# Spare weight tiles opened first, sixteen wide units inside a two-bank first part, fewer gathers in the projection, and a cheaper one-hot and id step in a decoder layer

## The chip, the cores and the metric

One core of one Trainium2 chip runs the kernel. The metric is device microseconds of an execution, the median of several runs. An execution of the program before takes 4138.65 us.

## What is computed

One decoder layer on 512 tokens of width 2048, all in float32: an RMS norm, two kinds of attention (16 heads each) with gates, a projection back to the residual, and a product-key expert layer. The parts that the change is about:

```
merged = concat(y_a, y_b) * sigmoid(gates)                  # 512 x 4096, 32 heads of 128
x  = x + merged @ w_out                                     # w_out 4096 x 2048
h  = rms_norm(x, ffn_norm_g)
q  = h @ w_peer_q                                           # 8 expert heads, two halves of 128 each
s1, i1 = top_k(q[first half]  @ sub_keys, 16)               # over 128 keys
s2, i2 = top_k(q[second half] @ sub_keys, 16)
cand = s1[:, None] + s2[None, :]                            # 16 x 16 candidates
top, pos = top_k(cand, 16);  expert = 128 * i1[..] + i2[..] # one of 16384 experts
g  = softmax(top);  a = u[expert] . h                       # u, v: 16384 x 2048
x  = x + sum over the 8 * 16 experts of (g * gelu(a)) * v[expert]
```

## The kernel before, in words

A float32 product runs as three matmuls of a rounded high part and a rest (`mm3`, lines L137 to L139). Each weight is loaded by SP in tiles of 512 KB (`load`, L101). A tile has two halves of 128x512. Of each half ACT writes the high part (`half_hi`, L108) and DVE the rest (`half_lo`, L113). Tiles live in a pool of three raw buffers, and `spare` opens two or more raw buffers beside them, with output tiles of their own. Pools are stacked in memory, so what a pool lies over depends on what was opened before it.

*Phase 1* norms the input, projects, and runs 32 attention heads. The last head's gate is stored to a scratch tensor in HBM by SP (`mrg`, L320).

*Phase 2* is the projection by w_out, in units of one half tile each. `out0_units` makes 128 narrow units for token block 0 (three matmuls of 512 columns each). `out_units` makes 128 wide units for blocks 1 to 3 (nine matmuls each), the list `main`. The list of units is run in order, the next half prepared while one is multiplied (`run`, with `LOOK`). The order is: the narrow units with `FEW` = 4 wide ones among the last of them; the norm of block 0 (L732 is its first DVE instruction), `WAIT` = 6 wide units, the query projection of block 0 with one wide unit after every 8 of its 64 units; then `select` for block 0, and the other wide units. From there on expert rows of block 0 are gathered. Each half adds `RATE` to a credit, and a full credit issues a gather: an indirect DMA of 128 rows of 8 KB by POOL (L952) into one of three buffers, and a product with a sum on DVE (L954). The last `REST` wide units come without gathers. After each issue a scheduler decides where an instruction goes in its engine's order.

*Phase 3* norms blocks 1 to 3 (hb, L872), transposes them (L878), splits them (L94, L95), projects the queries and selects the experts, four times (`select`). Within `select`, per half, an is_equal of 1536 elements (L839), a multiplication with the ids (L841) and a sum (L843) turn the chosen positions into ids. The last of the four is followed by nine transposes into `lists` (L1018). During the last part the first 32 units of the up projection run (`up_stream`, 12 matmuls of 336 columns each): 14 rows of 4 units are made ahead.

*Phase 4* treats 336 tokens of blocks 1 to 3 by dense products over all experts. `gate_matrix` builds the gate matrix in 84 groups of four tokens. Per group `pick` writes four one-hot rows for the first id (a three-row is_equal, L1029, and one tensor_scalar, L1031, that multiplies by the gate at once), four for the second id (L1033), and ACT scales three rows (L1035). PE multiplies (L1048), ACT copies (L1049), and every fourth group POOL copies (L1051). `LEFT` = 21 up units are spread over the groups, and 3 more follow. Its order on PE, DVE, ACT and POOL is written by hand. Then a stream of 948 weight halves carries the other up units, the down units and the gathers that are left: 352 in all.

Of the kernel before, what the change touches and what calls it, by code (L numbers as in the profile page):

```python
# [19 lines left out]
P = 128  # L20
SEQ = 512
# [45 lines left out]
RATE = 0.46  # L67
REST = 10
# [5 lines left out]
FEW = 4  # L74
# [3 lines left out]
LEFT = 4 * AHEAD - FIRST - 3  # L78
# [3 lines left out]
class Kern:  # L82
# [437 lines left out]
    def phase1(self):  # L520
        tc, nc, a = self.tc, self.nc, self.a
        with self.pool(name="hT", bufs=1, side="right") as hp, self.pool(name="keep", bufs=1) as keep, \
# [9 lines left out]
            with self.pool(name="xin", bufs=1) as xp:  # L532
# [8 lines left out]
                for k in range(KD):  # L541
# [3 lines left out]
                                                   op0=OP.mult, op1=OP.subtract)  # L545
                    a_, eng = (accp, nc.gpsimd) if k % 2 else (acc, nc.vector)
# [17 lines left out]
    def phase2(self, res, sm):  # L564
# [12 lines left out]
        with self.pool(name="mgr", bufs=1) as self.mgr, self.pool(name="msp", bufs=3) as self.msp, \  # L577
                self.pool(name="tka", bufs=1) as tk, self.spare(NRAW2, NSP2), \
# [109 lines left out]
    def out0_units(self, tk, main):  # L688
# [14 lines left out]
        def unit(w, c, q, u, k2):  # L703
            k = q * 8 + 2 * u + k2
            if k == 0:
                ps[c] = (self.pa if c < 2 else self.accp).tile([P, SEQ], F32, name="pa" if c < 2 else "acc")
# [4 lines left out]
        def some(qs):  # L711
            return [self.piece(a["w_out"][q, c, u], k2, st, lambda w, c=c, q=q, u=u, k2=k2: unit(w, c, q, u, k2))
                    for c in range(4) for q in qs for u in range(4) for k2 in range(2)]
# [5 lines left out]
        early, late = some(range(3)), some([3])  # L719
# [3 lines left out]
        out = early[:40] + [self.bare(own)] + early[40:64] + half(0) + early[64:] + [self.bare(bring, 3)]  # L723
        for i in range(0, len(late), 8):
            out += late[i:i + 8] + main[i // 8:i // 8 + 1] + (half(1) if i == 8 else [])
        return out
# [78 lines left out]
    def select(self, tk, vals, ids, n, gt, ie, eqs):  # L805
# [4 lines left out]
        nc.vector.tensor_copy(idf, ids)  # L810
        cand = tk.tile([P, n, NC // 8, 8], F32, name="cand")
# [25 lines left out]
        nc.vector.tensor_tensor(out=pf[:, 1], in0=slot, in1=w, op=OP.add)  # L837
        for c, eq in enumerate(eqs):
            nc.vector.tensor_tensor(out=eq, in0=pf[:, c, :, :, None].to_broadcast(bc),  # L839
                                    in1=iota[:, None, None, :].to_broadcast(bc), op=OP.is_equal)  # L840
            nc.vector.tensor_tensor(out=eq, in0=eq, in1=idf[:, c, :, None, :].to_broadcast(bc), op=OP.mult)  # L841
        for c, eq in enumerate(eqs):
            nc.vector.tensor_reduce(out=ie[:, c], in_=eq.rearrange("p (t h) a b -> p t h a b", t=nt), op=OP.add, axis=AX)  # L843
# [165 lines left out]
    def gate_matrix(self, pool, acc, ahead):  # L1009
        nc = self.nc  # L1010
        lists = pool.tile([P, 3, TD], F32, name="lists")
        for b in range(ND):
            for j in range(3):
# [4 lines left out]
                nc.scalar.copy(lists[:, j, b * P + o - NX:b * P + P - NX], tp[:, o:])  # L1018
# [270 lines left out]
```

## Time and profile before

| | |
|---|---|
| median of three runs | 4138.65 us (4133.84 to 4142.6) |
| the profiled execution | 4135.6 us, of which 4133.8 us is the span |
| PE busy | 4026.1 us (97%), 22575 matmuls |
| DVE busy | 3140.7 us (76%) |
| ACT busy | 1897.5 us (46%) |
| POOL busy | 644.4 us (16%) |
| DMA | 937.94 MB, mean 227 GB/s |

The span runs from the first to the last instruction of the trace. A stage of the program is found in it by the names of its instructions: the last head ends and the narrow units begin near 1454 us, block 0's norm is at 1587, the first hb at 1914, the end of the last `select` at 2151, the gate matrix from 2162 to 2287, and the stream of phase 4 after that. Busy shares are an average over stages with different limits, so the stages are read one by one. A window's row gives busy time of each engine, the granted TensorE clock as a share of 2.4 GHz, and what the DMA engines moved.

### The profile page before, as it was taken

What the parts mean: (1) busy time and instruction counts of PE and PEld (TensorE: products, weight loads), DVE (VectorE), ACT (ScalarE), POOL (GpSimd) and SP (SyncE); (2) the same over time, 40 slices, a digit from 0 to 9 for tenths busy, and PEclk for the clock granted to TensorE, in tenths of its full rate; (3) what the DMA queues carried; (4) which work ended last, traced back from release to release, by engine and by line L of the source; (5) the groups of instructions that cost most, each with busy time, mean ns of one, the idle gap of its engine ahead of it and who ended that gap; (6) DMA issues with size and microseconds to landing.
All of it is one profiled execution on the core that took longest, in us unless ns stands there. A gap on an engine that the chain in (4) does not pass through costs nothing. (4 is left out here: it accounts for less than half of the span.)

```text
span 4133.8 us, 61120 instructions
## 1 busy us (share of the span) xinstructions
PE 4026.1 (97%) x22575; PEld 3637.5 (88%) x22575; DVE 3140.7 (76%) x5379; ACT 1897.5 (46%) x3677; POOL 644.4 (16%) x531
## 2 busy tenths in 40 slices
PE   8999999999999989998999999999999999999999
PEld 6888888888888757787999999999999999999998
DVE  8555655655565567898999888888888888888886
ACT  4555555555555565433349433333333333333332
POOL 1111101111111100021001112112222222122220
PEclk9999999999999989998999999999999999999999
DMA  3222222222222377698337898989989989899896
GB/s 133 90 77 82 81 86 82 82 79 86 86 82 79 107 278 259 246 354 309 108 108 222 325 343 329 346 330 350 341 329 340 345 335 344 344 325 357 319 342 215
DMA packets 246925, 937.94 MB, mean 227 GB/s; under 512 B 23761, under 2 KB 70865, under 8 KB 197841
## 3 DMA queue, kind: packets, MB, share of 16 engines
q1 hardware_dynamic: 190944, 550.11, 38.3%
q0 software_dynamic: 52160, 375.94, 24.0%
q10 hardware_dynamic: 3520, 7.98, 0.6%
q8 instruction: 177, 2.90, 0.3%
q14 instruction: 124, 1.01, 0.1%
HBM read 895.75 MB, written 38.14 MB: 226 GB/s over the span
## 5 line engine op out<-in xcount | busy, mean ns | idle before, releaser
L108 ACT CAST whi<-raw 128x512 fp32r<-128x512 f32 x1820 | 1110.2, 621 | 1730.6 <-PE acc L138 604.2
L113 DVE TENSOR_TENSOR wlo<-raw,whi 128x512 fp32r<-128x512 f32 x1820 | 1219.6, 687 | 512.7 <-ACT whi L108 481.0
L137 PE MATMUL acc<-Wh,whi 128*128 128x336 f32 x2048 | 643.2, 318 | 5.7 <-DVE x L1124 3.0
L138 PE MATMUL acc<-Wl,whi 128*128 128x336 f32 x2048 | 645.1, 316 | 0.0
L137 PE MATMUL a<-dh,whi 128*128 128x336 f32 x1984 | 629.2, 317 | 0.8 <-issue 0.6
L138 PE MATMUL a<-dl,whi 128*128 128x336 f32 x1984 | 626.5, 316 | 0.0
L139 PE MATMUL a<-dh,wlo 128*128 128x336 f32 x1984 | 621.2, 316 | 0.6 <-DVE wlo L113 0.6
L139 PE MATMUL acc<-Wh,wlo 128*128 128x336 f32 x2048 | 608.5, 318 | 11.3 <-DVE wlo L113 10.8
L137 PE MATMUL mm<-hh,whi 128*128 128x512 f32 x1424 | 571.6, 402 | 8.6 <-ACT hh L543 8.6
L138 PE MATMUL mm<-hl,whi 128*128 128x512 f32 x1424 | 571.1, 401 | 4.3 <-DVE hl L544 4.0
L139 PE MATMUL mm<-hh,wlo 128*128 128x512 f32 x1424 | 569.9, 401 | 0.0
L137 PEld LDWEIGHTS acc<-Wh,whi 128*128 128x128 f32 x2048 | 385.4, 189 | 9.3 <-issue 5.7
L139 PEld LDWEIGHTS acc<-Wh,wlo 128*128 128x128 f32 x2048 | 376.1, 189 | 17.8 <-DVE wlo L113 17.5
L138 PEld LDWEIGHTS acc<-Wl,whi 128*128 128x128 f32 x2048 | 386.9, 189 | 0.0
L137 PEld LDWEIGHTS a<-dh,whi 128*128 128x128 f32 x1984 | 372.6, 188 | 2.2 <-issue 1.7
L138 PEld LDWEIGHTS a<-dl,whi 128*128 128x128 f32 x1984 | 372.8, 188 | 0.0
L139 PEld LDWEIGHTS a<-dh,wlo 128*128 128x128 f32 x1984 | 371.2, 188 | 1.1 <-DVE wlo L113 1.1
L138 PEld LDWEIGHTS mm<-hl,whi 128*128 128x128 f32 x1424 | 269.4, 189 | 71.7 <-DVE hl L544 9.8
L137 PEld LDWEIGHTS mm<-hh,whi 128*128 128x128 f32 x1424 | 270.1, 190 | 68.5 <-ACT hh L543 8.6
L139 PEld LDWEIGHTS mm<-hh,wlo 128*128 128x128 f32 x1424 | 269.5, 189 | 61.1 <-issue 0.5
L954 DVE CUSTOM_DVE_ANT_0 rows<-rows,h 128x2048 f32<-128x2048 f32 x128 | 292.1, 2283 | 12.5 <-DMA rows<-u,eidx 12.5
L966 DVE SCALAR_TENSOR_TENSOR x<-rows,aa,x 128x2048 f32<-128x2048 f32 x128 | 300.1, 2345 | 0.0
(393 smaller groups left out, 6136.8 us busy)
## 6 DMA issues: line engine op xcount, KB each, us to landing
raw<-ut SPq DMA_DIRECT2D x256, 512.0 KB
raw<-vt SPq DMA_DIRECT2D x256, 512.0 KB
raw<-w_in SPq DMA_DIRECT2D x178, 512.0 KB
raw<-w_out SPq DMA_DIRECT2D x128, 512.0 KB
raw<-w_pq SPq DMA_DIRECT2D x64, 512.0 KB
gd<-rows SPq DMA_DIRECT2D x21, 1024.0 KB
G<-gd SPq DMA_DIRECT2D x15, 1344.0 KB
raw<-w_up SPq DMA_DIRECT2D x24, 512.0 KB
```

Source lines behind the costliest of these rows:

```text
L108: self.nc.scalar.copy(hi, src)
L113: ins = self.nc.vector.tensor_tensor(out=lo, in0=src, in1=hi.bitcast(F32), op=OP.subtract)
L137: nc.tensor.matmul(out, wh, xh, start=start, stop=False)
L138: nc.tensor.matmul(out, wh, xl, start=False, stop=False)
L139: nc.tensor.matmul(out, wl, xh, start=False, stop=stop)
L954: nc.vector.tensor_tensor_reduce(out=row, in0=row, in1=self.h0, scale=1.0, scalar=0.0, op0=OP.mult, op1=OP.add, accum_out=self.aa[:, k:k + 1])
L966: nc.vector.scalar_tensor_tensor(out=self.x1[0], in0=row, scalar=self.aa[:, k:k + 1], in1=self.x1[0], op0=OP.mult, op1=OP.add)
```

## The change

Six edits. (1) The spare raw and split pools of phase 2 are opened ahead of its other pools. (2) The narrow units take output columns 0 and 1 first and then 2 and 3, all accumulated in the two banks of the pool `pa`; `FEW` goes from 4 to 16, and these wide units stand one after every sixth narrow unit from the 37th on. (3) `RATE` goes from 0.46 to 0.40 and `REST` from 10 to 14. (4) In `gate_matrix` the is_equal covers two rows, POOL writes the fourth and DVE the third by a tensor_scalar, ACT scales two; the transposes go by list and not by block, with an up unit after the second and the third list; `LEFT` goes from 21 to 16. (5) `select` finds ids as the minimum of a distance: DVE subtracts, ACT takes the absolute value, DVE takes the minimum. (6) In phase 1 the squares come in a loop of their own after the splits.

```diff
-RATE = 0.46
-REST = 10
+RATE = 0.40
+REST = 14
-FEW = 4
+FEW = 16
-LEFT = 4 * AHEAD - FIRST - 3
+LEFT = 4 * AHEAD - FIRST - 8
@@ phase1
                     nc.vector.scalar_tensor_tensor(out=hlo[:, k], in0=xt[:, k], scalar=g, in1=hh[:, k].bitcast(F32),
                                                    op0=OP.mult, op1=OP.subtract)
+                for k in range(KD):
                     a_, eng = (accp, nc.gpsimd) if k % 2 else (acc, nc.vector)
@@ phase2
-        with self.pool(name="mgr", bufs=1) as self.mgr, self.pool(name="msp", bufs=3) as self.msp, \
-                self.pool(name="tka", bufs=1) as tk, self.spare(NRAW2, NSP2), \
+        with self.spare(NRAW2, NSP2), self.pool(name="mgr", bufs=1) as self.mgr, \
+                self.pool(name="msp", bufs=3) as self.msp, self.pool(name="tka", bufs=1) as tk, \
@@ out0_units
-                ps[c] = (self.pa if c < 2 else self.accp).tile([P, SEQ], F32, name="pa" if c < 2 else "acc")
+                ps[c] = self.pa.tile([P, SEQ], F32, name="pa")
...
-        early, late = some(range(3)), some([3])
+        early, late = some(range(2), range(3)), some(range(2), [3]) + some(range(2, 4), range(4))
         for q in range(3):
             bring(q)
         half = lambda i: [self.bare(self.merged_half, 0, i)]
-        out = early[:40] + [self.bare(own)] + early[40:64] + half(0) + early[64:] + [self.bare(bring, 3)]
-        for i in range(0, len(late), 8):
-            out += late[i:i + 8] + main[i // 8:i // 8 + 1] + (half(1) if i == 8 else [])
-        return out
+        out, todo = [], main[:FEW]
+        for i, f in enumerate(early + late):
+            if i == len(early):
+                out.append(self.bare(bring, 3))
+            if i in (8, 28):
+                out += half(i // 20)
+            if i == 40:
+                out.append(self.bare(own))
+            out.append(f)
+            if i >= 36 and i % 6 == 0 and todo:
+                out.append(todo.pop(0))
+        return out + todo
@@ select
+        nc.vector.scalar_tensor_tensor(out=idf.rearrange("p s n k -> p (s n) k"), scalar=2.0 * NKEY,
+                                       in0=iota[:, None, :].to_broadcast([P, 2 * n, TOPK]),
+                                       in1=idf.rearrange("p s n k -> p (s n) k"), op0=OP.mult, op1=OP.add)
...
+        nc.vector.tensor_scalar(out=pf, in0=pf, scalar1=2.0 * NKEY, scalar2=None, op0=OP.mult)
         for c, eq in enumerate(eqs):
             nc.vector.tensor_tensor(out=eq, in0=pf[:, c, :, :, None].to_broadcast(bc),
-                                    in1=iota[:, None, None, :].to_broadcast(bc), op=OP.is_equal)
-            nc.vector.tensor_tensor(out=eq, in0=eq, in1=idf[:, c, :, None, :].to_broadcast(bc), op=OP.mult)
+                                    in1=idf[:, c, :, None, :].to_broadcast(bc), op=OP.subtract)
+            nc.scalar.activation(eq, eq, AF.Abs)
         for c, eq in enumerate(eqs):
-            nc.vector.tensor_reduce(out=ie[:, c], in_=eq.rearrange("p (t h) a b -> p t h a b", t=nt), op=OP.add, axis=AX)
+            nc.vector.tensor_reduce(out=ie[:, c], in_=eq.rearrange("p (t h) a b -> p t h a b", t=nt), op=OP.min, axis=AX)
@@ gate_matrix
-        for b in range(ND):
-            for j in range(3):
+        for j in range(3):
+            for b in range(ND):
...
+            if j:
+                next(ahead)
...
-            nc.vector.tensor_tensor(out=o1[:, :3], in0=lists[:, 0, t0:t0 + 3, None].to_broadcast(b3),
-                                    in1=iota[:, None, :].to_broadcast(b3), op=OP.is_equal)
-            nc.vector.tensor_scalar(out=o1[:, 3], in0=iota, scalar1=lists[:, 0, t0 + 3:t0 + 4],
-                                    scalar2=lists[:, 2, t0 + 3:t0 + 4], op0=OP.is_equal, op1=OP.mult)
+            nc.vector.tensor_tensor(out=o1[:, :2], in0=lists[:, 0, t0:t0 + 2, None].to_broadcast(b2),
+                                    in1=iota[:, None, :].to_broadcast(b2), op=OP.is_equal)
+            for i, eng in ((3, nc.gpsimd), (2, nc.vector)):
+                eng.tensor_scalar(out=o1[:, i], in0=iota, scalar1=lists[:, 0, t0 + i:t0 + i + 1],
+                                  scalar2=lists[:, 2, t0 + i:t0 + i + 1], op0=OP.is_equal, op1=OP.mult)
...
-            for i in range(3):
+            for i in range(2):
                 nc.scalar.activation(o1[:, i], o1[:, i], AF.Copy, scale=lists[:, 2, t0 + i:t0 + i + 1])
```

How the order of SP moves at the end of phase 1. `gate_12487` is the last head's gate, whose store waits for DVE; raw_13375 and raw_13389 are the two spare tiles, the other raws are of the pool of three. In brackets stands whose signals a load waits for. Before:

```order
L101 DMA raw_13262<-w_in 128x1024 [waits DMAHW6_50,DMAHW1_50,DVE_50]
L320 DMA mrg_82<-gate_12487 128x512 [waits DVE_50]
L101 DMA raw_13405<-w_out 128x1024 [waits DMAHW7_50,DMASW0_50,DVE_50]
L101 DMA raw_13421<-w_out 128x1024 [waits DMAHW0_50,DMASW1_50,DVE_50]
L101 DMA raw_13437<-w_out 128x1024 [waits DMAHW1_50,DMAHW5_50,DMASW2_50,DVE_50]
L101 DMA raw_13485<-w_out 128x1024 [waits DMAHW3_50,DVE_50]
L101 DMA raw_13375<-w_out 128x1024 [waits PE_50,Pool_50]
L101 DMA raw_13389<-w_out 128x1024 [waits DMASW5_50,DMAHW2_50,DMASW4_50,DVE_50]
```

and with the change:

```order
L101 DMA raw_13262<-w_in 128x1024 [waits DMAHW6_50,DMAHW1_50,DVE_50]
L320 DMA mrg_82<-gate_12487 128x512 [waits DVE_50]
L101 DMA raw_13375<-w_out 128x1024 [waits Pool_50]
L101 DMA raw_13389<-w_out 128x1024 [waits PE_50]
L101 DMA raw_13405<-w_out 128x1024 [waits DMAHW5_50,DMAHW7_50,DMASW0_50,DVE_50]
L101 DMA raw_13421<-w_out 128x1024 [waits DMAHW0_50,DMASW1_50,DVE_50]
```

The two spare tiles go from the fifth and sixth load of w_out to the first and second, and their waits no longer name a DMA.

The order of PE there. y_13188 is the last head's output, y_13007 that of the head before it, and pa_13385 the first accumulator of the narrow units. Before, no narrow unit stands ahead of the last head's last product:

```order
L306 MATMUL T_13222<-cst_63,P3_13182 128x128 [waits PE_50]
L315 MATMUL y_13188<-PTh1_13224,fv3_13126 128x128 [waits Activation_50]
L137 MATMUL pa_13385<-whi_13377,m0_13356 128x512 [waits Activation_50]
L138 MATMUL pa_13385<-wlo_13379,m0_13356 128x512 [waits DVE_50]
L139 MATMUL pa_13385<-whi_13377,m0_13356 128x512
```

and with the change:

```order
L306 MATMUL T_13041<-cst_63,P3_13001 128x128 [waits PE_50]
L137 MATMUL pa_13385<-whi_13377,m0_13356 128x512 [waits Activation_50]
L315 MATMUL y_13007<-PTh1_13043,mv3_11726 128x128 [waits Activation_50]
L490 MATMUL T_13119<-cst_63,raw_13117 128x128 x4
L138 MATMUL pa_13385<-wlo_13379,m0_13356 128x512 [waits DVE_50]
L139 MATMUL pa_13385<-whi_13377,m0_13356 128x512
L137 MATMUL pa_13385<-whi_13381,m0_13356 128x512
L138 MATMUL pa_13385<-wlo_13383,m0_13356 128x512 [waits DVE_50]
L139 MATMUL pa_13385<-whi_13381,m0_13356 128x512
```

The first narrow unit moved ahead of the last product of the head before the last, and 19 narrow units now stand ahead of the last head's last product.

The order of DVE at the start of phase 3, where hb and dl are the normed rows and the rest of their transposes. Before:

```order
L872 SCALAR_TENSOR_TENSOR hb_15449<-x13_13322,n1y_17338,hb_15449 128x512 [waits DVE_50]
L872 SCALAR_TENSOR_TENSOR hb_15449<-x13_13322,n1y_17338,hb_15449 128x512 x2
L954 ISA rows_14510,aa_85<-rows_14510,h0_14511 128x2048 [waits DMASW0_50]
L954 ISA aa_85 128x1
L954 ISA rows_14510,aa_85<-rows_14510,h0_14511 128x2048 [waits DMASW1_50]
L954 ISA aa_85 128x1
L95 TENSOR_TENSOR dl_17323<-tp_17351,dh_17322 128x384 [waits Activation_50]
```

and with the change (there L885 is the old L872, and L967 the old L954):

```order
L885 SCALAR_TENSOR_TENSOR hb_15642<-x13_13322,n1y_17316,hb_15642 128x512 [waits DVE_50]
L885 SCALAR_TENSOR_TENSOR hb_15642<-x13_13322,n1y_17316,hb_15642 128x512 x2
L967 ISA rows_14704,aa_85<-rows_14704,h0_14705 128x2048 [waits DMASW4_50]
L967 ISA aa_85 128x1
L95 TENSOR_TENSOR dl_17301<-tp_17329,dh_17300 128x384 [waits Activation_50]
L95 TENSOR_TENSOR dl_17301<-tp_17335,dh_17300 128x384 [waits Activation_50]
```

Nine gathered products stood after the first hb and 32 before it; now one stands after it and 28 before it, so 29 of the 352 gathers are done ahead of phase 4 where 41 were.

## Rows read from the trace of the kernel before

**Rows 1.** Stages by windows: from:to, length, busy per engine (instructions), clock, DMA share, GB/s
```profile
0.00:35.00 35.00, 22.12 (x50) 13.86 (x51) 28.38 (x36) 21.45 (x36) 16.10 (x15) 1.00 0.55 204
1433.00:1470.00 37.00, 19.65 (x56) 12.64 (x55) 16.48 (x29) 13.73 (x30) 3.46 (x4) 0.58 0.54 185
1470.00:1588.00 118.00, 109.44 (x437) 78.48 (x436) 91.81 (x148) 82.03 (x147) 0.91 (x1) 1.00 0.90 315
...
1710.00:1905.00 195.00, 192.66 (x827) 154.53 (x826) 167.72 (x227) 66.52 (x118) 39.50 (x32) 1.00 0.83 312
1905.00:1965.00 60.00, 43.80 (x215) 39.19 (x214) 50.37 (x70) 17.43 (x37) 9.26 (x9) 0.80 0.81 308
1965.00:2143.00 178.00, 171.95 (x1037) 169.32 (x1035) 171.79 (x744) 69.06 (x125) 0.00 (x0) 0.98 0.37 116
2162.00:2286.00 124.00, 122.44 (x907) 118.46 (x907) 122.98 (x269) 123.92 (x357) 15.12 (x20) 0.99 0.72 208
2286.00:2320.00 34.00, 28.70 (x168) 28.18 (x168) 24.84 (x43) 14.01 (x29) 6.54 (x8) 0.90 1.00 371
2320.00:4130.00 1810.00, 1792.99 (x11569) 1776.90 (x11568) 1514.22 (x1909) 672.35 (x1194) 376.65 (x317) 1.00 0.89 331
```

**Rows 2.** Timeline of SP's queue, 1415 to 1470: start, length, what is issued
```profile
1423.68 0.33 SPq L320 DMA_DIRECT2D mrg<-gate  x1
1434.15 34.91 SPq L101 DMA_DIRECT2D raw<-w_out  x9
```

**Rows 3.** SP's waits in the same stretch: us in total, times, longest
```profile
SPq L101 <- DMA mrg<-gate: 16.2, 1, 16.2
```

**Rows 4.** Timeline of PE: the first matmul of the third narrow unit
```profile
1465.38 0.79 PE L137 MATMUL pa<-whi,m 128*128 128x512 f32 x1 [6.56 <-ACT whi L108]
```

**Rows 5.** The line of block 0's norm, first instruction: its starts
```profile
L732 DVE TENSOR_REDUCE n0r<-ss x1: 158/158/158, 1587.2 to 1587.2; 128x1 f32<-128x4 f32 x1
```

**Rows 6.** Lines of DVE by shape, 1910 to 1965: busy, mean ns, idle before
```profile
L954 DVE CUSTOM_DVE_ANT_0 rows<-rows,h 128x2048 f32<-128x2048 f32 x10 | 22.8, 2284 | 4.0 <-DMA rows<-u,eidx 4.0
```

**Rows 7.** Timelines of DVE and ACT at the last selection and the lists
```profile
2136.49 0.20 DVE L836 TENSOR_SCALAR sw<-sw 128x96 f32<-128x96 f32 x1
2139.06 1.75 DVE L841 TENSOR_TENSOR hb<-hb,idf 128x1536 f32<-128x1536 f32 x1
2160.41 0.35 DVE L1031 TENSOR_SCALAR o<-cst,lists 128x128 f32<-128x128 f32 x1 [8.07 <-ACT lists L1018]
2154.34 5.64 ACTq L922 DMA_DIRECT2D idxx<-idx  x9
```

**Rows 8.** Lines by shape in the gate matrix, 2162 to 2285
```profile
L1035 ACT ACTIVATE o<-o,lists 128x128 f32<-128x128 f32 x250 | 91.8, 509 | 0.1
...
L1033 DVE TENSOR_TENSOR o<-lists,cst 128x512 f32<-128x512 f32 x83 | 56.4, 679 | 0.0
...
L1029 DVE TENSOR_TENSOR o<-lists,cst 128x384 f32<-128x384 f32 x82 | 45.3, 552 | 0.8 <-ACT o L1035 0.5 <-issue 0.2
```

**Rows 9.** Timeline of all engines within one group of the gate matrix
```profile
2205.35 0.68 DVE L1033 TENSOR_TENSOR o<-lists,cst 128x512 f32<-128x512 f32 x1
...
2205.40 1.26 POOL L1051 COPY G<-rows 128x128 f32<-128x128 f32 x1 [4.66 <-ACT rows L1049]
...
2205.95 0.55 DVE L1029 TENSOR_TENSOR o<-lists,cst 128x384 f32<-128x384 f32 x1
2206.42 0.34 DVE L1031 TENSOR_SCALAR o<-cst,lists 128x128 f32<-128x128 f32 x1
...
2206.68 0.68 DVE L1033 TENSOR_TENSOR o<-lists,cst 128x512 f32<-128x512 f32 x1
```

**Rows 10.** Two POOL lines over the span: minimum, median and maximum ns, starts
```profile
L1051 POOL COPY G<-rows x21: 293/605/1331, 2169.4 to 2287.6; 128x128 f32<-128x128 f32 x21
L264 POOL TENSOR_SCALAR raw<-raw x32: 1486/1657/2047, 165.8 to 1436.1; 128x512 f32<-128x512 f32 x32
```

**Rows 11.** The chain that ended last, behind the gate matrix: start, length, what
```profile
2286.27 11.04 DMA raw<-vt
```

**Rows 12.** Lines of DVE by shape in the stream of phase 4, 2300 to 4130
```profile
L113 DVE TENSOR_TENSOR wlo<-raw,whi 128x512 fp32r<-128x512 f32 x964 | 641.2, 686 | 221.5 <-ACT whi L108 215.6 <-issue 0.9 <-PE a L139 0.8
```

More of the change, by code (lines that the diff above doesn't have):

```diff
@@ L709, in unit, with some @@
                 self.residual(ps[c], 0, c, True)
-        def some(qs):
+        def some(cs, qs):
             return [self.piece(a["w_out"][q, c, u], k2, st, lambda w, c=c, q=q, u=u, k2=k2: unit(w, c, q, u, k2))
-                    for c in range(4) for q in qs for u in range(4) for k2 in range(2)]
+                    for c in cs for q in qs for u in range(4) for k2 in range(2)]
         def own():
@@ L1021, in gate_matrix @@
         it = iota[:, None, :].to_broadcast(bc)
-        b3 = [P, 3, NKEY]
+        b2 = [P, 2, NKEY]
         def pick(g):
```

## Prediction

> **What bounds the kernel now.** I read the stages by windows first [rows 1], because PE is busy in 97% of the span and only the stages in which it is not can give time. Four of them matter. At the end of phase 1 (1433 to 1470) PE is busy 19.65 of 37 us, at a granted clock of 0.58, which is near the lower of its two levels. In the first part of the projection (1470 to 1588) it is busy 109.44 of 118 us, while the DMA engines run at 0.90 and 315 GB/s. Between the projection and phase 3 (1905 to 1965) it is busy 43.80 of 60 us. In phase 3 and in the gate matrix DVE is full: 171.79 of 178 and 122.98 of 124 us. In the rest of the projection (1710 to 1905) and in phase 4 PE is full, and there a change pays only if it takes matmuls out of the stage.
>
> Then the queues. SP issues the last head's store at 1423.68, and the next thing it issues, the first load of w_out, comes at 1434.15 [rows 2]. In that stretch it waited 16.2 us for a transfer of that gate [rows 3]. The third narrow unit starts at 1465.38, after 6.56 us in which PE waited for a cast [rows 4], so the narrow units begin with too few tiles. Block 0's norm, the end of the first part, is at 1587.2 [rows 5].
>
> The sum is made against the profiled execution, 4135.6 us; the median is 3.05 us above it.
>
> **Squares last.** The splits of phase 1 are issued ahead of the squares, but the scheduler's order moves little. PE is idle 12.9 of the first 35 us [rows 1], so a fraction of that could come or go either way. I count 0, bounds -5 and +3.
>
> **Spare tiles first, and the two-bank order.** Before, both spare tiles stand behind four loads into the pool of three, and the second waits for the gate's store, because its memory lay over tiles that the last head still used. Now they come first and wait for no DMA. PE has 19 narrow units ahead of the last head's last product where it had none.
>
> The work of the first part: at 192.66 us for 827 matmuls [rows 1] a matmul of 512 columns takes 0.233 us, a narrow unit 0.70 and a wide one 2.10. Then 128 narrow units and 16 wide ones are 90 + 33.6 = 123 us of PE. If they began at about 1437 beside the last head's few matmuls (some 4 us), PE alone would end at 1564. The transfers: 37 x 185 + 117 x 315 GB/s is 43.7 MB from 1433 to 1587 [rows 1], and twelve more wide units are six tiles, 3.1 MB more, so 46.8 MB. At 315 GB/s from 1424 that ends at 1573. The later end decides, and with the first tiles still few I take 1577. So block 0's norm comes 10 us earlier, and 12 wide units, 12 x 2.10 = 25 us of PE, are done ahead of it instead of in the stage after, which PE fills. That is **-35 us**. From below the gain is 9: no earlier start, and the 25 us of PE go into the 118 - 109.4 = 8.6 us that PE was idle. From above it is 48: PE bounds throughout.
>
> The two banks cost nothing that I can see: the wide units take the other six, three for each column, and the narrow ones now never hold them. One wait can arise, the first of column 2 on the residual add of column 0 on DVE, one add of 0.7 us that stands two columns behind.
>
> **Fewer gathers.** Of 41 gathers ahead of phase 4, 29 are left, and after the first hb only one of nine. Each product takes DVE 2.28 us, with 4.0 us of waits for ten of them [rows 6]. DVE stands there between hb, the transposes' splits and PE. Eight go, 18.3 us of DVE, with most of the waits. PE was idle 16.2 us of those 60 [rows 1], and not all of it was DVE's doing: weight tiles have to arrive too, at a DMA share of 0.81. I take **-12**, bounds 0 and -22 (all eight and all waits).
>
> The 12 gathers go into the stream of phase 4: 12 x 2.28 = 27 us of DVE, of which DVE has 1810 - 1514 = 296 us idle, and 12.6 MB, 38 us at 331 GB/s, where 0.11 of 1810 us, 199 us, is free [rows 1]. DVE's idle time before the halves' rests is put down to casts [rows 12], so it is slack and no queue. I take **+4**; the ends are 0 and +27, all of DVE's time exposed.
>
> **Ids by a minimum.** Per half of a selection, two passes over 1536 elements of 1.75 us become one [rows 7], and ACT, which has time in phase 3 (69 of 178 us), takes the absolute value. Two small DVE instructions are added, of 0.2 us (192 and 96 elements) to 0.4. So a selection saves DVE 3.5 - 0.6 = 2.9 us, three of them within the stage that DVE fills: 8.7. The last selection sits on the chain to the lists; there one pass of DVE becomes one of ACT, about no change. DVE then waits 8.07 us for the lists, of which ACT spends 5.64 issuing nine small DMAs [rows 7]; the two up units put among the transposes give PE some 3.7 us of work there, which is taken off the gate stage below. Together **-8**, bounds 0 and -14. The selection of block 0 lies beside wide units and counts 0.
>
> **One-hot rows.** From start to start DVE spends 0.60 + 0.47 + 0.26 = 1.33 us on a group [rows 9]. Two rows instead of three: 0.47 less the step of 0.13 per 128 columns is 0.34, and the sum 1.20. Over 84 groups that is 11 us, and five up units less are ten halves less at 0.6 us, 6 us more. ACT loses one scaling of three, 30 of its 91.8 us [rows 8]. So the stage would go from 124 to about 107. POOL's own work hides: its row is a tensor_scalar of a quarter of the width of the nearest one, 1.49 us [rows 10], an estimate of 0.4 us in a group of 1.20. But POOL beside DVE is not free. The copy that takes 293 ns at best [rows 10] took 1.26 us when it began 0.05 us after DVE's two-input is_equal, and it ended with DVE's tensor_scalar under way; DVE kept its spacing [rows 9]. Now POOL must get in 84 times and not 21. If each delays DVE by the 0.15 us that its 0.4 sticks out of the tensor_scalar's 0.26, 13 us are given back. I take half of that: the stage -10. Behind it three more up units (5.5 us) run, but PE waits there anyway for tiles of the down weights, 11.04 us in the chain [rows 11]. That leaves **-6**, bounds -13 and +12.
>
> The Trainium skill speaks against this edit: the page "SBUF — State Buffer", section "SBUF: two separate sides", has GpSimd and a DVE instruction with two SBUF inputs hold a shared port pair as an exclusive lock for a whole instruction, whichever starts first, the other fully blocked. The copy of rows 9 agrees for POOL as the one that is blocked; no row shows DVE blocked here in the gate matrix. What it would make of the time is the second rival.
>
> **Sum.** 0 - 35 - 12 + 4 - 8 - 6 = -57, so 4078.6 for a profiled execution and, 3.05 higher, about **4082 us**.
>
> **Rivals.** (1) *The first part gains little.* The early tiles only move the wait, and DMA and PE together bound it: -9 instead of -35, and the transition -6. Sum -9 - 6 + 4 - 8 - 6 = -25, **4114**. For it speaks that DMA and PE are both near full there, at shares of 0.90 and 0.93; against it the 16.2 us wait and the clock of 0.58, which both go if work lies ahead of them. (2) *POOL becomes the bound of the gate matrix*, the other side. If its tensor_scalar took the 1.49 us of the nearest row and held DVE off all that time, a group would take 1.20 - 0.26 + 1.49 = 2.43 us, 84 x 1.10 = 92 us more than before; with the others, -51 + 92 = +41, **4180**. It decides from 51/84 + 0.13 = 0.74 us per group that POOL adds to DVE. Against it: four times fewer columns than that row, and the copy of the same size at 0.29 to 1.33 us never moved DVE. By the rule of the Trainium skill's page, with the 0.4 us in series in every group, the stage would take 107 + 34 = 141 us, and the whole 4105. (3) *The moved gathers are paid in phase 4*, all 27 us: -57 + 23 = -34, **4105**; for it, that stage's DMA share of 0.89, against it DVE's idle time there. (4) *Nothing changes*, 4139: what is gained early is awaited again at the first tiles of the down weights.
>
> **Chances.** Forecast 0.80, rival 1 0.07, rival 2 0.05, rival 3 0.06, rival 4 0.02. Below, the first part and the transition at their better ends give another 22 us: 4060. Above, rival 3 is inside and rival 1 at the edge: 4112. A measurement tells 0.2%, 8 us, from no change. Faster 0.80 + 0.07 + 0.06 = 0.93, same 0.02, slower 0.05.
>
> **What will show it.** Right: w_out loads from about 1424 without a gap of 10 us; narrow units before 1454; block 0's norm near 1577; the first hb some 35 us before 1914 and one gathered product behind it; the gate matrix in 110 to 118 us, POOL's tensor_scalar near 0.4 us (longer where it began under an is_equal); in phase 4 a DMA share near 0.91 and PE still full. Wrong: a norm after 1585; idle time of DVE or PE put down to POOL in the gate matrix; waits for gathered rows or rests in phase 4 beyond some 10 us.

## The result

The changed kernel takes 4095.32 us (median of four runs, 4090.29 to 4099.38) against 4136.24 us (4131.89 to 4142.6) for the kernel before, beside it. The ratio is 0.9899, 95% interval 0.9881 to 0.9918, so it is 1.0% faster. Run once more, beside three of the experiments, it was 4094.24 against 4132.01, a ratio of 0.9907 (0.9891 to 0.9924). The profiled execution took 4090.29 us, 45.3 less than the profiled one of before. Forecast was 4082 us, 57 less, within a range of 4060 to 4112.

### The profile page after: what moved, and what is told of

It is laid out like the page before. It is cut to its first block, busy times and chain, and to the rows that moved or that the text cites. A ratio compares the mean times of both kernels' runs of the same rounds, so it can differ in the third digit from the quotient of the medians.

```text
span 4088.5 us, 61203 instructions
## 1 busy us (share of the span) xinstructions
PE 4004.4 (98%) x22575; PEld 3623.8 (89%) x22575; DVE 3118.8 (76%) x5379; ACT 1887.8 (46%) x3603; POOL 738.5 (18%) x615
## 5 line engine op out<-in xcount | busy, mean ns | idle before, releaser
L139 PE MATMUL acc<-Wh,wlo 128*128 128x336 f32 x2048 | 597.8, 318 | 16.9 <-DVE wlo L113 16.0
L967 DVE CUSTOM_DVE_ANT_0 rows<-rows,h 128x2048 f32<-128x2048 f32 x128 | 292.1, 2283 | 2.5 <-DMA rows<-u,eidx 2.5
```

Source lines behind the costliest of these rows:

```text
L139: nc.tensor.matmul(out, wl, xh, start=False, stop=stop)
L967: nc.vector.tensor_tensor_reduce(out=row, in0=row, in1=self.h0, scale=1.0, scalar=0.0, op0=OP.mult, op1=OP.add, accum_out=self.aa[:, k:k + 1])
```

## The profile after

Where the time went is seen in PE's own stages. PE's idle time in a stretch is worked out here as its length less the sum over its matmuls of the pace from start to start when nothing is waited for: 0.2325 us for 512 columns, 0.1725 for 384, 0.153 for 336, 0.119 for 256, 0.111 for 128, each read from the trace. Time lost because PE runs at the lower of its two clock levels counts as idle here too. By this both kernels hold 3915.5 us of matmuls, and the idle time fell from 218.3 to 173.0 us, which is the whole 45.3 us.

| stretch | before: length (idle) | changed: length (idle) |
|---|---|---|
| start to the last head's store | 1423.7 (43.9) | 1420.8 (41.0) |
| store to the norm of block 0 | 163.5 (45.4) | 161.9 (21.7) |
| to the norm of blocks 1 to 3 | 325.4 (20.9) | 304.7 (22.3) |
| the 47 us behind it | 47.0 (21.1) | 47.0 (10.6) |
| to the end of the last selection | 192.0 (12.7) | 167.6 (5.5) |
| to the first one-hot row | 8.8 (6.1) | 12.6 (0.8) |
| gate matrix | 126.2 (14.7) | 118.7 (15.1) |
| the 40 us behind it | 40.0 (8.7) | 40.0 (5.5) |
| the stream of phase 4 | 1807.2 (44.8) | 1815.3 (50.5) |

Windows of the changed kernel, with the columns and the stages of [rows 1]:

```profile
1430.00:1467.00 37.00, 30.30 (x134) 23.49 (x133) 32.80 (x56) 28.93 (x57) 3.48 (x4) 0.95 0.90 318
1467.00:1583.00 116.00, 110.83 (x449) 83.82 (x450) 84.83 (x144) 71.80 (x129) 0.91 (x1) 0.99 0.86 302
...
1880.00:1940.00 60.00, 51.63 (x282) 47.78 (x281) 39.21 (x73) 23.26 (x49) 1.15 (x1) 0.89 0.55 191
1940.00:2097.00 157.00, 154.16 (x944) 152.11 (x944) 156.19 (x725) 70.71 (x118) 0.00 (x0) 1.00 0.39 118
...
2116.00:2233.00 117.00, 114.05 (x852) 107.58 (x851) 114.83 (x264) 105.74 (x267) 116.49 (x105) 1.00 0.76 214
2233.00:2280.00 47.00, 43.94 (x274) 43.12 (x274) 39.04 (x63) 19.12 (x36) 8.42 (x9) 0.96 0.97 355
2280.00:4085.00 1805.00, 1782.29 (x11497) 1764.51 (x11495) 1526.23 (x1916) 661.03 (x1187) 378.52 (x327) 1.00 0.90 337
```

The tail of phase 1 is full of matmuls (134 where there were 56) at a clock of 0.95 instead of 0.58. The clock tells the same as the idle time: where PE had little to do the stretch's clock was near half of 2.4 GHz, and now it is near the whole. In the gate matrix POOL, busy 15.12 of 124 us before, is now busy 116.49 of 117.

The timeline of SP's queue at the end of phase 1, then the two norms and the first narrow matmul, to be held against [rows 2, 5]:

```profile
1420.76 0.33 SPq L320 DMA_DIRECT2D mrg<-gate  x1
1421.42 25.60 SPq L101 DMA_DIRECT2D raw<-w_out  x11
...
L741 DVE TENSOR_REDUCE n0r<-ss x1: 134/134/134, 1582.7 to 1582.7; 128x1 f32<-128x4 f32 x1
L741 DVE TENSOR_REDUCE n1r<-ss x1: 159/159/159, 1887.4 to 1887.4; 128x3 f32<-128x12 f32 x1
...
1436.06 0.78 PE L137 MATMUL pa<-whi,m 128*128 128x512 f32 x1
```

The first w_out load follows the store by 0.7 us where it took 10.5, the first narrow matmul starts at 1436 and not 1454.66, and yet block 0's norm comes at 1582.7 and not at the 1577 forecast.

The lines of the gate matrix by shape, 2116 to 2233, with the columns of [rows 8]:

```profile
L1047 POOL TENSOR_SCALAR o<-cst,lists 128x128 f32<-128x128 f32 x84 | 106.4, 1277 | 233.2 <-DMA idxx<-idx 233.2
L1064 PE MATMUL acc<-o,o 128*128 128x128 f32 x669 | 88.7, 284 | 3.0 <-POOL o L1047 3.0
...
L1049 DVE TENSOR_TENSOR o<-lists,cst 128x512 f32<-128x512 f32 x83 | 57.7, 696 | 0.0
...
L1047 DVE TENSOR_SCALAR o<-cst,lists 128x128 f32<-128x128 f32 x83 | 30.6, 369 | 0.0
L1067 POOL COPY G<-rows 128x128 f32<-128x128 f32 x20 | 11.0, 550 | 0.2
```

POOL's row takes 1.277 us where 0.4 was estimated. 84 of them and 21 copies of 0.55 us are 118.8 us, the stage's 118.7. DVE's instructions grew by some 0.02 to 0.03 us each.

## The experiments

Each is the changed kernel with one edit; the run with the old list of narrow units and the last one have two. Medians of four runs (eight in the first) stand beside the kernel before on the same chip; stretches and marks are of the profiled execution. One profile is not the rule: in nine profiles of kernels whose first part is that of the changed kernel, block 0's norm comes between 1582.7 and 1589.5 us, the changed kernel's own profile being the earliest.

### The spare tiles alone

```diff
-        with self.spare(NRAW2, NSP2), self.pool(name="mgr", bufs=1) as self.mgr, \
-                self.pool(name="msp", bufs=3) as self.msp, self.pool(name="tka", bufs=1) as tk, \
+        with self.pool(name="mgr", bufs=1) as self.mgr, self.pool(name="msp", bufs=3) as self.msp, \
+                self.pool(name="tka", bufs=1) as tk, self.spare(NRAW2, NSP2), \
```

> The changed kernel with the spare pools opened after the other pools of phase 2, as before. Marks of the changed kernel's profile: last head's store 1420.8 us, block 0's norm 1582.7, norm of blocks 1 to 3 1887.4. Theory 1 (the early tiles fill the tail of the last head): SP waits some 16 us for a gate transfer again, no narrow unit runs ahead of the last head's end, store to block 0's norm grows from 161.9 by 13 to 18 us, and the total by as much (about 4110). Theory 2 (the wide units placed in the first part give the gain, and the tail is bound by its own casts): that stretch grows by less than 5 us, the total stays within 5 us.

4120.39 us, ratio 0.9971 (0.9960 to 0.9982). SP's queue and wait, and block 0's norm, in this run:

```profile
1422.37 0.33 SPq L320 DMA_DIRECT2D mrg<-gate  x1
1432.84 38.72 SPq L101 DMA_DIRECT2D raw<-w_out  x11
...
SPq L101 <- DMA mrg<-gate: 16.0, 1, 16.0
...
L741 DVE TENSOR_REDUCE n0r<-ss x1: 134/134/134, 1609.9 to 1609.9; 128x1 f32<-128x4 f32 x1
```

The wait of 16 us is back, and store to norm is 187.5 us against 161.9, more than theory 1 had it (13 to 18). PE's idle time there is 46.6 us, against 45.4 before and 21.7 changed. So the placement of two tiles is worth some 25 us by itself, and the other edits of this stage together are worth nothing there.

### The sixteen wide units, and the order by columns

```diff
-FEW = 16
+FEW = 4
```

> The changed kernel with 4 wide units within the first part in place of 16. Theory 1 (the first part is bound by PE's work, with small waits): store to block 0's norm, 161.9 us, shrinks by about 25 us (12 x 2.10), the next stretch of 304.7 us grows by as much, total within 3 us. Theory 2 (the first part is bound by transfers or by the making of the halves, and wide units fill PE's waits): it shrinks by 10 to 15 only, and the total grows by 10 to 15.

4085.55 us (4085.05 to 4085.99), ratio 0.9887 (0.9870 to 0.9903). The norms:

```profile
L741 DVE TENSOR_REDUCE n0r<-ss x1: 137/137/137, 1563.2 to 1563.2; 128x1 f32<-128x4 f32 x1
L741 DVE TENSOR_REDUCE n1r<-ss x1: 159/159/159, 1883.3 to 1883.3; 128x3 f32<-128x12 f32 x1
```

The first norm comes 19.5 us earlier, the stretch between the norms is 15.4 longer. PE's idle time in the first part is 23.2 us with 4 wide units and 21.7 with 16: twelve more of them filled 1.5 us. That is not told from nothing, because the nine profiles with 16 have 21.7 to 26.0 us there. Theory 2 falls. Theory 1 is nearer, but between the norms the idle time is 15.1 and not 22.3 (14.0 to 16.1 in the three profiles of changed kernels with 4 wide units, 19.0 to 22.3 in the nine with 16), so the early wide units cost more there than they filled. By the ratios (0.9899 and 0.9907 for the changed kernel) the total is 5 to 8 us lower, which neither theory had, and the intervals overlap. Nor was the start of this stage full of PE in the kernel before, 1588 to 1710:

```profile
1588.00:1710.00 122.00, 113.92 (x496) 88.79 (x495) 98.96 (x315) 64.12 (x114) 0.00 (x0) 0.97 0.72 247
```

The second edit put the old list of narrow units back, with 4 wide units in it.

```diff
-FEW = 16
+FEW = 4
-        early, late = some(range(2), range(3)), some(range(2), [3]) + some(range(2, 4), range(4))
+        early, late = some(range(3)), some([3])
...
-            if i >= 36 and i % 6 == 0 and todo:
-                out.append(todo.pop(0))
-        return out + todo
+        out = early[:40] + [self.bare(own)] + early[40:64] + half(0) + early[64:] + [self.bare(bring, 3)]
+        for i in range(0, len(late), 8):
+            out += late[i:i + 8] + main[i // 8:i // 8 + 1] + (half(1) if i == 8 else [])
+        return out
```

> The changed kernel with the old list of narrow units (all columns, three quarters of the rows first, then the rest) and 4 wide units among the last. Theory 1 (the two-bank order by itself costs and brings nothing): as the run with 4 wide units in the new order, within 3 us at block 0's norm and in the total. Theory 2 (the order by columns starts PE earlier or frees banks for the wide units): over 5 us slower than that run.

4085.76 us, ratio 0.9890 (0.9873 to 0.9906): the same time as the run before. The first norm comes at 1569.5 us, 6.3 later than with the new order, so theory 1 does not hold at the norm, but the total shows nothing of it. Its second norm comes at 1888.4, no earlier than in the changed kernel; what it gains on that kernel lies behind it, most in phase 4 (1851.3 us behind the gate matrix, against 1855.3).

### Where the early wide units cost

In the changed kernel PE stands still from 1742 to 1748. Its row, and ACT's wait between 1690 and 1760:

```profile
1747.81 1.65 PE L137 MATMUL acc<-whi,mh 128*128 128x512 f32 x3 [5.20 <-ACT whi L108]
...
ACT mh L94 <- DMA m<-mrg: 10.4, 2, 8.6
...
1747.80:1753.00 5.20, 5.19 (x12) 4.08 (x13) 5.20 (x8) 1.61 (x3) 1.15 (x1) 0.50 0.12 16
```

The last row is the window behind the hole: PE is busy all through it, but at a granted clock of 0.50, the lower of its two levels, after 5.4 us without work. Twelve matmuls take the 5.2 us, where 2.8 would do at 0.2325 us each, so the hole costs over 7 us and not only the wait. A wait of 2.0 to 6.5 us stands at this place in all ten profiles with 16 early wide units, and in none of the three changed kernels with 4.

ACT stands 8.6 us before the cast of the next half of merged values, 768 KB, and the casts for PE's next units stand behind it. In the run with 4 wide units the same load took 14.1 us, but ACT waited 0.8; it had weight halves to cast, six of them between the load's issue and the cast that needs it, where the changed kernel had four:

```profile
ACT mh L94 <- DMA m<-mrg: 0.8, 1, 0.8
```

Just ahead of the load the changed kernel issues two of its three loads of 1 MB for hb. An edit was to move them:

```diff
+            self.run(main[done:done + 16])
             for t in range(ND):
                 nc.scalar.dma_start(self.hb[:, t], a["gffn"])
-            self.run(main[done:-REST])
+            self.run(main[done + 16:-REST])
```

> The changed kernel itself once more, beside the next three on one chip. Every theory: about 0.990 of the kernel before, some 4092 to 4096 us, a hole of about 7 us in PE's work near 1742.

> The changed kernel with the three loads of 1 MB for hb issued after the next 16 wide units and not ahead of them. Theory 1 (with 16 wide units early, the load of the next half of merged values stands right behind these loads, ACT waits 8.6 us for it and PE has no unit left): the hole near 1742 shrinks from 7.2 us to under 3, the stretch between the two norms from 304.7 to about 300, total 3 to 6 us faster than the changed kernel. Theory 2 (the early wide units are missing as cover for the selection of block 0, whatever is loaded): the hole stays, total within 2 us.

With the edit: 4092.10 us, ratio 0.9898 (0.9881 to 0.9914); without it, on the same chip: 4094.24, 0.9907 (0.9891 to 0.9924). The two intervals overlap. The hole stays, and ACT's wait with it (8.5 us):

```profile
1750.60 1.65 PE L137 MATMUL acc<-whi,mh 128*128 128x512 f32 x3 [5.27 <-ACT whi L108]
```

But the edit did not move the loads. It moves them in the program's text, and the scheduler put them back. First the changed kernel, then the run with the edit; the two loads stand 4.25 and 2.05 us ahead of the load of merged values in both, and at the same places in ACT's order:

```profile
1726.17 0.34 ACTq L602 DMA_DIRECT2D hb<-gffn  x1
1728.37 0.33 ACTq L602 DMA_DIRECT2D hb<-gffn  x1
1730.42 0.38 SPq L624 DMA_DIRECT2D m<-mrg  x1
...
1728.42 0.33 ACTq L603 DMA_DIRECT2D hb<-gffn  x1
1730.62 0.33 ACTq L603 DMA_DIRECT2D hb<-gffn  x1
1732.67 0.38 SPq L625 DMA_DIRECT2D m<-mrg  x1
```

So this run decides nothing between the two theories, and the theory of the hb loads is untested. That PE lacks units there fits theory 2 and the run with 4 wide units, where the same two loads also stand ahead (7.9 and 4.9 us), and the kernel before, where ACT waited 8.3 us for such a load and PE lost under 2; it is argued and not shown. Why the load takes 14 to 16 us is not settled either; the first three gathers of 1 MB go with it in each of these runs.

### The gathers

```diff
-RATE = 0.40
-REST = 14
+RATE = 0.46
+REST = 10
```

> The changed kernel with 0.46 gathers a half and 10 units without them. Theory 1 (gathered products held the start of phase 3, and phase 4 has room for them): from the norm of blocks 1 to 3 to the first one-hot row, 227.2 us, grows by about 10 to 12 us, and phase 4 behind the gate matrix, 1855.2 us, shrinks by about 4 to 5; total slower by 5 to 8. Theory 2 (the gathers cost the same wherever they are): both move by the same, total within 2 us.

4095.81 us, ratio 0.9910 (0.9893 to 0.9926). It is less than an undoing: with 12 wide units fewer behind the selection only 35 gathers came ahead of phase 4 (28 ahead of the first hb, 7 behind it), not the 41 of before. For those six, the 47 us behind the second norm have 13.9 us of idle PE, against 10.6 and 8.3 in the two profiles of the changed kernel: 3 to 6 us. The total does not show it. The direction is theory 1's, the size half of it. Phase 4 behind the gate matrix took 1856.9 us where 1855.3 was measured, not 4 to 5 less; kernels with the same phase 4 lie between 1854.6 and 1862.6 us in their profiles, so a few us there cannot be read from one.

What did grow in phase 4 is what PE waits for DVE's rests of the halves. Behind the gate matrix, first in the kernel before and then in the changed one:

```profile
PE acc L139 <- DVE wlo L113: 10.8, 14, 1.8
...
PE acc L139 <- DVE wlo L113: 16.0, 21, 1.5
PE a L139 <- DVE wlo L113: 3.2, 4, 0.9
```

With 0.2 on the up units before, that is 19.2 us for 11.0; DVE's time there was not all slack. With 34 gathers done ahead (4 wide units) these waits are 13.0 to 14.8 us, but with 35 done ahead in this run they are 21.1, so the number of gathers alone does not set them.

### The ids

```diff
-                                    in1=idf[:, c, :, None, :].to_broadcast(bc), op=OP.subtract)
-            nc.scalar.activation(eq, eq, AF.Abs)
+                                    in1=iota[:, None, None, :].to_broadcast(bc), op=OP.is_equal)
+            nc.vector.tensor_tensor(out=eq, in0=eq, in1=idf[:, c, :, None, :].to_broadcast(bc), op=OP.mult)
```

> The changed kernel with the ids found as before (comparison, multiplication and sum on DVE). Theory 1 (phase 3 is bound by DVE, three selections by 2.9 us): from the norm of blocks 1 to 3 to the first one-hot row, 227.2 us, grows by 8 to 11 us and the total by as much. Theory 2 (PE's work and tiles bound phase 3 and the selections hide): within 3 us.

From the second norm to the first one-hot row it took 236.8 us against 227.2, 9.6 more, as theory 1 had it. Phase 3 in this run (window 1940 to 2110), and the row of DVE ahead of the lists:

```profile
1940.00:2110.00 170.00, 163.05 (x987) 159.93 (x986) 168.56 (x722) 64.71 (x116) 0.00 (x0) 0.99 0.38 115
...
2124.49 0.69 DVE L113 TENSOR_TENSOR wlo<-raw,whi 128x512 fp32r<-128x512 f32 x1 [7.73 <-ACT whi L108]
```

DVE is full in both kernels, and PE's idle time in phase 3 is 12.6 us with the old ids, as before, and 5.5 with the new: 7.1 of the 9.6 us. From the end of the last selection to the first one-hot row it is 5.0 us here and 0.8 with the new ids. The median, 4097.39 (4091.4 to 4109.09), ratio 0.9907 (0.9891 to 0.9924), is too wide to show 9 us.

### The one-hot rows

The old rows, with the new number of up units:

```diff
-            nc.vector.tensor_tensor(out=o1[:, :2], in0=lists[:, 0, t0:t0 + 2, None].to_broadcast(b2),
-                                    in1=iota[:, None, :].to_broadcast(b2), op=OP.is_equal)
-            for i, eng in ((3, nc.gpsimd), (2, nc.vector)):
...
+            nc.vector.tensor_tensor(out=o1[:, :3], in0=lists[:, 0, t0:t0 + 3, None].to_broadcast(b3),
+                                    in1=iota[:, None, :].to_broadcast(b3), op=OP.is_equal)
+            nc.vector.tensor_scalar(out=o1[:, 3], in0=iota, scalar1=lists[:, 0, t0 + 3:t0 + 4],
+                                    scalar2=lists[:, 2, t0 + 3:t0 + 4], op0=OP.is_equal, op1=OP.mult)
```

> The changed kernel with the one-hot rows written as before (DVE three rows by one comparison and one by a tensor_scalar, ACT scaling three, POOL none), 16 up units among the groups kept. Theory 1 (POOL's rows now bound the gate matrix at 1.39 us a group, so the edit paid little): DVE bounds at 84 x 1.33 + 16 x 0.6 = 121 us, against 118.7 with POOL; total 0 to 4 us slower. Theory 2 (POOL is hidden and the stage is bound elsewhere, the edit paid its 11 us): the stage takes about 130 us, total 8 to 12 slower.

4098.96 us, ratio 0.9916 (0.9899 to 0.9932). The gate matrix took 123.1 us, against 121 of theory 1 and 130 of theory 2. DVE and ACT are both full there (119.39 and 120.79 of 121 us). So the rows on POOL are worth 4.4 us of this stage.

Then POOL's copies went to ACT:

```diff
-                nc.gpsimd.tensor_copy(G[:, tb], st[:, :GR])
+                nc.scalar.copy(G[:, tb], st[:, :GR])
```

> The changed kernel with the copy of every fourth group into G on ACT in place of POOL. Theory 1 (POOL bounds the gate matrix, because each of its instructions takes one turn between DVE's, five turns for four groups): 21 instructions fewer on POOL, the stage goes from 118.7 to 113 to 115 us, where DVE's own work of about 114 bounds it, and PE's waits for POOL's rows (7.4 us) vanish; total 3 to 5 us faster. Theory 2 (POOL's busy time is not what bounds the stage): 118 us as now, total within 2.

4089.51 us, ratio 0.9895 (0.9879 to 0.9912); the stage takes 115.7 us, 3.0 less. Its window, 2116 to 2229:

```profile
2116.00:2229.00 113.00, 111.56 (x844) 105.89 (x843) 111.72 (x263) 107.29 (x285) 112.67 (x84) 1.00 0.78 221
```

Fewer instructions on POOL shorten the stage, so POOL was on its bound. But 21 copies of 0.55 us, 11.6 us of POOL, brought only 3.0: POOL's 84 rows now fill 112.67 us, 1.34 each, where they took 1.277. What the row costs depends on what DVE does beside it. POOL and DVE are now both full (112.67 and 111.72 of 113 us), and which of the two ends last this run does not tell. The waits for POOL's rows, of PE's matmuls and of its weight loads added up though they overlap, fell from 7.4 to 3.0 us and did not vanish.

Last, what POOL's row costs with less of DVE beside it:

```diff
-            nc.vector.tensor_tensor(out=o2, in0=lists[:, 1, t0:t0 + 4, None].to_broadcast(bc), in1=it, op=OP.is_equal)
+            if g < 3:
+                nc.vector.tensor_tensor(out=o2, in0=lists[:, 1, t0:t0 + 4, None].to_broadcast(bc), in1=it, op=OP.is_equal)
```

> The changed kernel leaving out the four-row comparison for the second id from the fourth group on (the first three groups' rows are used again), so DVE has one two-input instruction of 256 columns a group and not a second one of 512. Theory 1 (POOL's tensor_scalar is stretched by waiting for DVE's two-input instructions): its median falls from 1.26 us to 0.4 to 0.8. Theory 2 (1.26 us is what POOL needs for 128 columns, near the 1.49 us for 512 columns in phase 1): it stays above 1.1 us.

This kernel leaves out a comparison that the result needs, and the profile is of its one execution. The line of the tensor_scalar on POOL here (minimum, median and maximum ns), and the stage:

```profile
L1050 POOL TENSOR_SCALAR o<-cst,lists x84: 782/924/1594, 2114.7 to 2220.9; 128x128 f32<-128x128 f32 x84
...
2116.00:2222.00 106.00, 104.14 (x854) 103.59 (x854) 67.49 (x184) 99.64 (x268) 89.43 (x105) 1.00 0.84 238
```

The median falls from 1.26 to 0.92 us, a value between the two theories: the least of the 84, 0.78 us, comes nearest to what POOL needs alone, and DVE's second two-input instruction adds 0.34 to the median. The stage falls to 107.4 us, where PE is nearly full (104.14 of 106 us).

### The squares

```diff
-                for k in range(KD):
                     a_, eng = (accp, nc.gpsimd) if k % 2 else (acc, nc.vector)
```

> The changed kernel with each square behind its own split in phase 1, as before. Theory 1 (the loop of squares gave the 2.9 us by which the last head's store came earlier): the store at 1423 to 1424 us instead of 1420.8, total 2 to 3 us slower. Theory 2 (that difference is one between executions): the store within 1 us, total within 1.5.

4095.33 us, ratio 0.9909 (0.9892 to 0.9926), and the store at 1421.01 us. The squares' loop gives nothing. The store's time varies over the profiles of this study, from 1420.6 to 1422.7 us with the loop, and 1423.7 in the one profile of before; what makes the 2.9 us was not found.

### Four wide units, and the copies on ACT

The edits of the two runs above together (`FEW = 4`, the copy on ACT).

> The changed kernel with 4 wide units early and the copy into G on ACT. Theory 1 (the two parts that lost or gave nothing lie in different stages): the gains of the single runs add, some 7 and 4 us, so 10 us below the changed kernel beside it, about 4083. Theory 2 (one takes the other's gain away): 4086 or above, or within 3 us of the changed kernel.

4077.40 us (4073.88 to 4079.33), ratio 0.9862 (0.9845 to 0.9878), the fastest kernel here. On the same chip the changed kernel took 4094.24 (4090.61 to 4099.64): 16.8 us less by medians, 13.7 by the spans of the two profiles, more than the 10 of theory 1. Of these, 2.9 are there at the second norm, 2.8 come in the gate matrix (115.9 us for 118.7) and 9.0 behind it (1848.5 us for 1857.5), with 1.1 given back in phase 3. With more wide units behind the selection, 34 gathers come ahead of phase 4 and not 29. That fits a shorter phase 4 (the other two kernels with 34 took 1854.6 and 1851.3 us). Against it stands the run with 35 gathers ahead and 16 wide units early, which took 1856.9 us there. So the 9 us are not shown to be the gathers', and what made them is open.

## Why the prediction was right, and where it was off

The sign and the range held; the sum was 12 us too good. Read by PE's idle time the terms below add to the 45.3 us measured. The sum came as near as it did partly by luck: the ids gave 4.5 us more than forecast and the start of the trace 2.9 that nobody forecast, and they cover part of a shortfall of 12.7 in the first part. By its terms:

- *Squares*: forecast 0, measured -2.9 in the profile, and by the run that undid them nothing.
- *Spare tiles and two-bank order*: forecast -35, measured -22.3 (-1.6 us in the length from store to norm, -20.7 between the norms; the idle time there gives the same). This is the mis-sized term. The mechanism of the tiles was right, and larger than I had it: 25 us. What failed is the step "12 wide units, 12 x 2.10 = 25 us of PE, are done ahead of it instead of in the stage after, which PE fills". I took them as filling time in which the first part waits for transfers. Once the tiles come early there is little such time: the wide units filled no idle time of PE that can be read from the profiles (1.5 us in this pair), they lengthened the first part by 21.0 us of their 25, and the norm, forecast at 1577, came at 1582.7 (1584.5 to 1589.5 in the eight other profiles with this first part). And the stage after was not full of PE: the row read for it [rows 1] begins at 1710, ahead of it PE was busy 113.92 of 122 us, and between the two norms the kernel before had 20.9 us of idle time. With 16 units moved ahead it was 7.2 us more than with 4, a hole near 1742. That the units left there were the cover of the selection fits this and is not shown. "The two banks cost nothing" held for the total.
- *Fewer gathers*: forecast -12, the 47 us behind the norm measured -10.5. Of it 3 to 6 us are shown to be the gathers', by a run that undid six of twelve; for the rest there is no run. In phase 4 +4 was forecast; the stream's idle time grew by 5.7, and PE's waits for DVE's rests by 8.2, so "slack and no queue" was not all true. That the gathers made them grow is not shown.
- *Ids*: forecast -8; phase 3 measured -7.2, and the run that undid them 9.6 with the lists. That the last selection gives "about no change" was too careful: from the last selection to the first one-hot row PE's idle time fell by 5.3 us. With the old ids and the two up units among the transposes it was 5.0, so 4.2 of the 5.3 are the ids' and about 1 the units'.
- *One-hot rows*: forecast -6, made of a stage 10 us shorter and 4 us given back. The stage is 7.5 us shorter, but its idle time is 15.1 us as before (14.7): what left it is work, 50 matmuls of 336 columns (7.7 us, some four of the five up units), and three units run behind it. PE's idle time behind it fell by 3.2. The step that failed is "an estimate of 0.4 us in a group of 1.20": it is 1.277, about one group of DVE, POOL is busy through the whole stage (84 x 1.277 + 21 x 0.55 us), and the rows on POOL gain 4.4 us over the old ones.

Rival 2 was right that POOL would come to bound the stage and wrong in how, and in its price: 1.41 us a group (118.7 over 84) and not 2.43. It had DVE held off by POOL; POOL was the one held off, and DVE kept a group of 1.25 us (the median from start to start), where 1.20 was worked out. The Trainium skill's page "SBUF — State Buffer" ("SBUF: two separate sides") has whoever comes second fully blocked. For POOL the run with less of DVE beside it agrees (0.92 us for 1.26); a DVE blocked for a whole instruction of POOL is in no row here, and the 141 us worked out from that rule were 118.7. Rival 1 (the first part gains little) was wrong about the tiles, which gave 25 us, and its small gain is true of the wide units alone. Rival 3 does not hold: the 12 moved gathers did not cost the 27 us of DVE's time in phase 4, where everything behind the gate matrix grew by 8.1 us, 5.5 of them the three up units. Rival 4 (nothing changes) does not hold either. In the range, the better ends of the first part and the transition are 13 and 10 us, 23 and not 22, which changes nothing.

Of the signs named, the early loads and narrow matmuls and phase 4's DMA share of 0.90 came as said. The first hb came 25 us earlier and not 35 (1889.1), the gate matrix at 118.7 lies just above 118, and POOL's row is far above 0.4. One sign of being wrong showed in the gate matrix, PE's waits for POOL's rows (3.0 us of the matmuls), and the waits for rests in phase 4 grew by 8.2, near the 10 that were set.

## What to carry to other kernels

Work moved into a stage gains only the idle time that it fills there, and it can take cover from the stage it leaves: before crediting moved units at their full length, look for the waits on both sides. Where a pool's memory lies decides when its first load may start; a queue whose first entry waits for memory of the stage before holds all behind it, and the fix is to put there what is free early. An engine that helps another is priced by a row of the same size and neighbours, and if there is none, by the nearest row undivided: the 1.49 us of four times the columns was nearer to the 1.277 measured than a quarter of it. Where a scheduler places the instructions, an edit of the program's text is no change until the trace shows the new order.

## What the runs showed of the hardware that was not expected

POOL's tensor_scalar of 128 columns takes 0.78 us at least (a comparison and a product), where one of 512 columns (a minimum alone) took 1.49 at least [rows 10]; so in these rows a quarter of the columns is half of the price. Beside a dense row of DVE's two-input instructions its median is 1.26 us, about one group of DVE, and with one of them left out 0.92. A load of 768 KB took 14 to 16 us from issue to the cast that waited for it, while three indirect loads of 1 MB, loads for hb just ahead of it and tiles of weights went with it, at 366 to 406 GB/s in sum. After 5.4 us without work PE's next twelve matmuls in the changed kernel ran at a granted clock of 0.50, 0.43 us apart and not 0.23.
